# Loading expert weights in 32 KB stretches, with x transposed ahead of all experts

## The chip, the cores and the metric

The kernel runs on one core of one Trainium2 chip. The metric is the device time of one execution in microseconds, the median of several runs. Three runs of the kernel before gave 196.9, 197.62 and 198.62 us.

## What is computed

Eight experts, each a layer of two matrix products with a relu between them:

```python
n_experts, capacity, hidden, expert_hidden = 8, 256, 512, 2048
x:  (8, 256, 512) float32    w1: (8, 512, 2048) float32    w2: (8, 2048, 512) float32

h = np.matmul(x, w1)
h = np.maximum(h, 0)
return np.matmul(h, w2).astype(np.float32)
```

Each expert's two weight matrices hold 4.19 MB apiece in float32; x is 0.52 MB for each expert, and so is the output.

## The kernel before

One Python loop runs over the eight experts. All loads are issued from POOL's queue (GpSimd), which converts float32 to bfloat16 on the way; the outputs leave by SP's queue. A planner of dependencies places the semaphores; within each engine the order is that of the program.

For each expert:

- x arrives as a tile of 128 partitions with two rows of 512 each (line 57; the two rows lie side by side in memory). Eight 128x128 transposes on TensorE (line 63) go through two PSUM buffers, and VectorE copies each one to `xt_sb` (line 68).
- w1 arrives in one DMA (line 74). Its view `e (kt p) n -> e p kt n` gives partition p the rows p, 128 + p, 256 + p and 384 + p: four separate runs of 8 KB each. w2 arrives in two halves (lines 78 and 79); by its view partition p gets sixteen separate rows of 2 KB. The pool `moe_big` has two buffers of each, so the loads of expert e+2 wait until expert e has been worked off.
- The first layer (line 85): 16 tiles of 128 hidden units, each from four matmuls that accumulate, w1 stationary (128x128) and `xt_sb` moving (256 columns). ScalarE applies the relu and writes `ht_sb` (line 92).
- The second layer: `ht_sb` is stationary and w2 moving (512 columns). For each of two row tiles, eight matmuls accumulate over the first half of the hidden units (line 103) and eight over the second (line 117), in banks of their own. ScalarE copies the first half's sum to `out_sb` (line 111), VectorE adds the second (line 125), and SP stores the expert's 512 KB (line 127).

The identity for the transposes is made on POOL ahead of the loop (line 51; its instructions carry the lines of a helper, masks.py).

Of the kernel before, what the change touches and what calls it, by code (L numbers as in the profile page):

```python
# [1 line left out]

# [5 lines left out]


@with_exitstack
def kernel(
    ctx: ExitStack,
    tc: tile.TileContext,
    x: bass.AP,
    w1: bass.AP,
    w2: bass.AP,
    out: bass.AP,
):
    nc = tc.nc  # L20
    P = 128

    n_experts, capacity, hidden = x.shape
    _, _, expert_hidden = w1.shape

    M = capacity
    K1 = hidden
    K2 = expert_hidden
    N2 = hidden

    assert M % P == 0 and K1 % P == 0 and K2 % P == 0
    M_TILES = M // P
    K1_TILES = K1 // P
    K2_TILES = K2 // P

    bf = mybir.dt.bfloat16
    f32 = mybir.dt.float32

    x_r = x.rearrange("e (p mt) k -> e p mt k", p=P)
    w1_r = w1.rearrange("e (kt p) n -> e p kt n", p=P)  # L40
    w2_r = w2.rearrange("e (kt p) n -> e p kt n", p=P)
    out_r = out.rearrange("e (p mt) n -> e p mt n", p=P)

    big = ctx.enter_context(tc.tile_pool(name="moe_big", bufs=2))
    small = ctx.enter_context(tc.tile_pool(name="moe_small", bufs=3))
    psum_tr = ctx.enter_context(tc.tile_pool(name="moe_psum_tr", bufs=2, space=bass.MemoryType.PSUM))
    psum_mm = ctx.enter_context(tc.tile_pool(name="moe_psum_mm", bufs=6, space=bass.MemoryType.PSUM))
    const = ctx.enter_context(tc.tile_pool(name="moe_const", bufs=1))

    identity = const.tile([P, P], bf, name="identity")  # L50
    make_identity(nc, identity)

    HALF = K2_TILES // 2

    for e in range(n_experts):
        x_sb = small.tile([P, M_TILES, K1], bf, tag="x", name="x_sb")
        nc.gpsimd.dma_start(x_sb[:], x_r[e])  # L57

        xt_sb = small.tile([P, K1_TILES, M], bf, tag="xt", name="xt_sb")
        for mt in range(M_TILES):  # L60
            for kt in range(K1_TILES):
                pt = psum_tr.tile([P, P], bf, tag="ps_tr", name="pt_tr")
                nc.tensor.transpose(  # L63
                    pt[:],
                    x_sb[:, mt, kt * P:(kt + 1) * P],
                    identity[:],
                )
                nc.vector.tensor_copy(  # L68
                    xt_sb[:, kt, mt * P:(mt + 1) * P],
                    pt[:],  # L70
                )

        w1_sb = big.tile([P, K1_TILES, 16 * P], bf, tag="w1", name="w1_sb")
        nc.gpsimd.dma_start(w1_sb[:], w1_r[e])  # L74

        w2_a = big.tile([P, HALF, N2], bf, tag="w2a", name="w2_a")
        w2_b = big.tile([P, HALF, N2], bf, tag="w2b", name="w2_b")
        nc.gpsimd.dma_start(w2_a[:], w2_r[e, :, :HALF, :])  # L78
        nc.gpsimd.dma_start(w2_b[:], w2_r[e, :, HALF:, :])  # L79

        ht_sb = big.tile([P, K2_TILES, M], bf, tag="ht", name="ht_sb")
        for mt in range(K2_TILES):
            pt = psum_mm.tile([P, N2], f32, tag="ps_mm", name="pt_mm1")
            for kt in range(K1_TILES):
                nc.tensor.matmul(  # L85
                    pt[:, :M],
                    w1_sb[:, kt, mt * P:(mt + 1) * P],
                    xt_sb[:, kt, :],
                    start=(kt == 0),
                    stop=(kt == K1_TILES - 1),  # L90
                )
            nc.scalar.activation(  # L92
                ht_sb[:, mt, :], pt[:, :M],
                mybir.ActivationFunctionType.Relu,
            )

        out_sb = small.tile([P, M_TILES, N2], f32, tag="o", name="out_sb")
        pa = [None] * M_TILES
        pb = [None] * M_TILES
        for mt in range(M_TILES):  # L100
            pa[mt] = psum_mm.tile([P, N2], f32, tag="ps_mm", name="pt_mm2a")
            for kt in range(HALF):
                nc.tensor.matmul(  # L103
                    pa[mt][:],
                    ht_sb[:, kt, mt * P:(mt + 1) * P],
                    w2_a[:, kt, :],
                    start=(kt == 0),
                    stop=(kt == HALF - 1),
                )
        for mt in range(M_TILES):  # L110
            nc.scalar.activation(  # L111
                out_sb[:, mt, :], pa[mt][:],
                mybir.ActivationFunctionType.Identity,
            )
            pb[mt] = psum_mm.tile([P, N2], f32, tag="ps_mm", name="pt_mm2b")
            for kt in range(HALF):
                nc.tensor.matmul(  # L117
                    pb[mt][:],
                    ht_sb[:, HALF + kt, mt * P:(mt + 1) * P],
                    w2_b[:, kt, :],  # L120
                    start=(kt == 0),
                    stop=(kt == HALF - 1),
                )
        for mt in range(M_TILES):
            nc.vector.tensor_add(out_sb[:, mt, :], out_sb[:, mt, :], pb[mt][:])  # L125

        nc.sync.dma_start(out_r[e], out_sb[:])


# [1 line left out]
_INS = ['x', 'w1', 'w2']  # L131
_OUTS = [((8, 256, 512), 'float32')]


# [23 lines left out]
```

## Time and profile before

| | before |
|---|---|
| median of three runs | 197.62 us |
| the profiled execution's span | 197.5 us |
| its mean granted TensorE clock | 0.890 |
| TensorE matmuls, busy | 136.3 us (69%) |
| ScalarE, busy | 59.1 us |
| VectorE, busy | 22.4 us |
| load queue, share of 16 DMA engines | 99.8% |
| bytes read from HBM / written to HBM | 71.30 MB / 4.19 MB |

The profile is of one execution. Busy times of TensorE come from matmul records whose ends are modelled, so starts say more than durations. The rates of the windows count a load's bytes as they are written to SBUF, in bfloat16. A window's DMA share is the mean busy share of the 16 DMA engines; it can pass 1 because packets overlap. [...]

### The profile page before, as it was taken

How to read it: one execution, taken by the hardware profiler on the slowest of the kernel's cores; microseconds unless marked ns; L12 is line 12 of the kernel's file. 1: busy time of each engine (PE TensorE's matmuls, PEld its weight loads, DVE VectorE, ACT ScalarE, POOL GpSimd, SP SyncE). 2: the span in 40 equal slices, each digit the busy share in tenths (PEclk: the TensorE clock that was granted, in tenths of full speed). 3: DMA queues.
4: the chain of work that ended last, by engine and by line, in shares of the span. 5: the costliest groups of instructions: out<-in, count | busy, mean ns of one | idle time of the engine just before them, and what ended most of it. 6: DMA issues, size and time to landing. Idle time of an engine off the chain costs nothing.

```text
span 197.5 us, 2028 instructions
## 1 busy us (share of the span) xinstructions
PE 136.3 (69%) x824; PEld 87.9 (44%) x832; DVE 22.4 (11%) x80; ACT 59.1 (30%) x145; POOL 25.2 (13%) x38
## 2 busy tenths in 40 slices
PE   0304998159971999459970999519993699639990
PEld 0103853038530784248530684207741584227740
DVE  0200003100041000400040000500013000500011
ACT  2001741018400382018400382004720283005620
POOL 8700014000140002210230103100111000000000
PEclk9999999859997599969997599966999699966997
DMA  4999999999999999999999999999999999999402
GB/s 67 163 211 168 207 217 212 255 211 208 216 217 253 208 212 217 208 257 209 217 216 253 208 211 215 215 254 207 214 217 206 257 211 217 211 256 207 83 0 108
DMA packets 23177, 39.97 MB, mean 202 GB/s; under 512 B 640, under 2 KB 17024, under 8 KB 23168
## 3 DMA queue, kind: packets, MB, share of 16 engines
q0 software_dynamic: 22016, 35.65, 99.8%
q1 hardware_dynamic: 1152, 4.19, 5.6%
q8 instruction: 6, 0.10, 0.2%
q14 instruction: 3, 0.02, 0.0%
HBM read 71.30 MB, written 4.19 MB: 382 GB/s over the span
## 4 chain that ended last, share of the span: by engine, by line
DMA 72%; PE 13%; issue 10%; POOL 2%; DVE 0%; POOLq 0%; DVEq 0%
DMA w_sb<-in_w_dram 72%; PE pt_mm L85 9%; PE pt_mm2b L117 2%; PE pt_mm2a L103 2%; POOL x_sb L57 1%; POOL w_a L78 0%; POOL w_b L79 0%; POOL w_sb L74 0%; DVE out_sb L125 0%; POOL identity masks.py:199 0%; PE pt_tr L63 0%; POOL identity masks.py:197 0%; POOLq masks.py:199 0%; POOLq L74 0%; POOLq L78 0%
## 5 line engine op out<-in xcount | busy, mean ns | idle before, releaser
L85 PE MATMUL pt_mm<-xt_sb,w_sb 128*128 128x256 bf16 x512 | 72.7, 313 | 41.2 <-DMA w_sb<-in_w_dram 41.2
L85 PEld LDWEIGHTS <-w_sb 128*128 128x128 bf16 x512 | 56.6, 113 | 57.4 <-DMA w_sb<-in_w_dram 45.1
L92 ACT ACTIVATE ht_sb<-pt_mm 128x256 bf16<-128x256 f32 x128 | 48.3, 383 | 110.2 <-PE pt_mm L85 105.0
L117 PE MATMUL pt_mm2b<-w_b,ht_sb 128*128 128x512 bf16 x128 | 28.9, 379 | 0.0
L103 PE MATMUL pt_mm2a<-w_a,ht_sb 128*128 128x512 bf16 x120 | 28.5, 379 | 0.4
L125 DVE TENSOR_TENSOR out_sb<-out_sb,pt_mm2b 128x512 f32<-128x512 f32 x16 | 11.0, 688 | 126.7 <-PE pt_mm2b L117 118.9
L63 PE MATMUL pt_tr<-identity,x_sb 128*128 128x128 bf16 x64 | 12.1, 235 | 14.8 <-DVE xt_sb L68 9.6
L117 PEld LDWEIGHTS <-ht_sb 128*128 128x128 bf16 x128 | 12.5, 98 | 15.1
L103 PEld LDWEIGHTS <-ht_sb 128*128 128x128 bf16 x128 | 12.5, 98 | 13.4
L68 DVE COPY xt_sb<-pt_tr 128x128 bf16<-128x128 bf16 x64 | 12.0, 220 | 44.3 <-PE pt_tr L63 44.3
L74 POOL DMA_DIRECT2D w_sb<-in_w_dram x8 | 6.0, 754 | 80.0 <-PE pt_mm L85 80.0
L111 ACT ACTIVATE out_sb<-pt_mm2a 128x512 f32<-128x512 f32 x16 | 9.6, 597 | 19.8 <-PE pt_mm2a L103 19.8
L63 PEld LDWEIGHTS <-x_sb 128*128 128x128 bf16 x64 | 6.3, 105 | 18.3 <-issue 10.5
L78 POOL DMA_DIRECT2D w_a<-in_w_dram x8 | 7.1, 891 | 16.2 <-PE pt_mm2a L103 16.2
L79 POOL DMA_DIRECT2D w_b<-in_w_dram x8 | 7.1, 884 | 15.9 <-PE pt_tr L63 15.9
L57 POOL DMA_DIRECT2D x_sb<-in_x_dram x8 | 4.7, 582 | 12.1 <-PE pt_tr L63 11.7
L92 ACT ACT_TABLE_LOAD x1 | 1.3, 1283 | 0.7 <-PEq L142 0.7
masks.py:199 POOL TENSOR_SCALAR_AFFINE_SELECT identity<-identity 128x128 bf16<-128x128 bf16 x1 | 0.3, 304 | 0.1
masks.py:197 POOL MEMSET identity<- 128x128 bf16 x1 | 0.2, 204 | 0.3 <-POOLq L142 0.3
L142 POOL MEMSET const-float32-0.0<- 128x1 f32 x1 | 0.1, 98 | 0.2 <-issue 0.2
L142 POOL MEMSET const-bfloat16-1.0<- 128x1 bf16 x1 | 0.1, 101 | 0.0
L142 POOL MEMSET const-uint8-127<- 128x1 uint8 x1 | 0.1, 101 | 0.0
(1 smaller groups left out, 0.1 us busy)
## 6 DMA issues: line engine op xcount, KB each, us to landing
w_sb<-in_w_dram POOLq DMA_DIRECT2D x8, 2048.0 KB, 35.7
w_a<-in_w_dram POOLq DMA_DIRECT2D x8, 1024.0 KB, 38.1
w_b<-in_w_dram POOLq DMA_DIRECT2D x8, 1024.0 KB, 39.7
out_dram<-out_sb SPq DMA_DIRECT2D x8, 512.0 KB, 6.3
x_sb<-in_x_dram POOLq DMA_DIRECT2D x8, 256.0 KB, 37.0
```

Source lines behind the costliest of these rows:

```text
L57: nc.gpsimd.dma_start(x_sb[:], x_r[e])
L63: nc.tensor.transpose(pt[:], x_sb[:, mt, kt * P:(kt + 1) * P], identity[:],)
L68: nc.vector.tensor_copy(xt_sb[:, kt, mt * P:(mt + 1) * P], pt[:],)
L74: nc.gpsimd.dma_start(w1_sb[:], w1_r[e])
L78: nc.gpsimd.dma_start(w2_a[:], w2_r[e, :, :HALF, :])
L79: nc.gpsimd.dma_start(w2_b[:], w2_r[e, :, HALF:, :])
L85: nc.tensor.matmul(pt[:, :M], w1_sb[:, kt, mt * P:(mt + 1) * P], xt_sb[:, kt, :], start=(kt == 0), stop=(kt == K1_TILES - 1),)
L92: nc.scalar.activation(ht_sb[:, mt, :], pt[:, :M], mybir.ActivationFunctionType.Relu,)
L103: nc.tensor.matmul(pa[mt][:], ht_sb[:, kt, mt * P:(mt + 1) * P], w2_a[:, kt, :], start=(kt == 0), stop=(kt == HALF - 1),)
L111: nc.scalar.activation(out_sb[:, mt, :], pa[mt][:], mybir.ActivationFunctionType.Identity,)
L117: nc.tensor.matmul(pb[mt][:], ht_sb[:, HALF + kt, mt * P:(mt + 1) * P], w2_b[:, kt, :], start=(kt == 0), stop=(kt == HALF - 1),)
L125: nc.vector.tensor_add(out_sb[:, mt, :], out_sb[:, mt, :], pb[mt][:])
```

## The change

- The rows of each weight matrix go to the partitions in another order: `e (p kt) n -> e p kt n`, so partition p gets rows 4p to 4p+3 of w1 and rows 16p to 16p+15 of w2. Each partition then loads one contiguous stretch of 32 KB in float32 of either matrix. Every matrix comes in one DMA, but for the last expert's w2, which comes in four pieces of 6, 5, 3 and 2 row tiles.
- x is loaded whole, ahead of the weights: partition p gets sixteen consecutive rows, 32 KB. The identity is made on POOL after the first expert's loads have been issued.
- All 64 transposes run ahead of the experts, eight to a PSUM bank. Since hidden row p*4 + kt lies in partition p of tile kt, a transpose reads every fourth column of x (`kt::KT1`); VectorE and ScalarE take turns in copying eight transposes at once into `xt_sb`, which now holds all experts, with a permutation of the columns.
- By the same order the first layer reads its stationary tiles from w1 with a step of sixteen columns (`2 * g + i::KT2`). Two tiles of 256 columns share a bank, and the relu of 512 columns goes to ScalarE and VectorE in turn.
- The second layer accumulates all sixteen tiles in one bank for each row tile, the two row tiles alternating. VectorE copies one and ScalarE the other to `out_sb`. The last expert's output leaves in two halves, by SP's and ScalarE's queues.
- Four buffers of each weight matrix instead of two.

```diff
--- before.py
+++ after.py
@@ -1,4 +1,3 @@
-
 from contextlib import ExitStack
 
 import concourse.bass as bass
@@ -19,112 +18,111 @@
 ):
     nc = tc.nc
     P = 128
-
-    n_experts, capacity, hidden = x.shape
-    _, _, expert_hidden = w1.shape
-
-    M = capacity
-    K1 = hidden
-    K2 = expert_hidden
-    N2 = hidden
-
-    assert M % P == 0 and K1 % P == 0 and K2 % P == 0
-    M_TILES = M // P
-    K1_TILES = K1 // P
-    K2_TILES = K2 // P
-
     bf = mybir.dt.bfloat16
     f32 = mybir.dt.float32
 
-    x_r = x.rearrange("e (p mt) k -> e p mt k", p=P)
-    w1_r = w1.rearrange("e (kt p) n -> e p kt n", p=P)
-    w2_r = w2.rearrange("e (kt p) n -> e p kt n", p=P)
+    E, C, H = x.shape
+    F = w1.shape[2]
+    MT = C // P
+    KT1 = H // P
+    KT2 = F // P
+    J = E * C // P
+    PL = P // E
+    J2 = J // MT
+
+
+    x_r = x.rearrange("e c k -> (e c) k").rearrange("(p j) k -> p j k", p=P)
+    w1_r = w1.rearrange("e (p kt) n -> e p kt n", p=P)
+    w2_r = w2.rearrange("e (p kt) n -> e p kt n", p=P)
     out_r = out.rearrange("e (p mt) n -> e p mt n", p=P)
 
-    big = ctx.enter_context(tc.tile_pool(name="moe_big", bufs=2))
-    small = ctx.enter_context(tc.tile_pool(name="moe_small", bufs=3))
-    psum_tr = ctx.enter_context(tc.tile_pool(name="moe_psum_tr", bufs=2, space=bass.MemoryType.PSUM))
-    psum_mm = ctx.enter_context(tc.tile_pool(name="moe_psum_mm", bufs=6, space=bass.MemoryType.PSUM))
-    const = ctx.enter_context(tc.tile_pool(name="moe_const", bufs=1))
+    const = ctx.enter_context(tc.tile_pool(name="const", bufs=1))
+    wpool = ctx.enter_context(tc.tile_pool(name="weights", bufs=4))
+    hpool = ctx.enter_context(tc.tile_pool(name="hidden", bufs=2))
+    opool = ctx.enter_context(tc.tile_pool(name="outs", bufs=3))
+    ps_h = ctx.enter_context(tc.tile_pool(name="ps_h", bufs=4, space=bass.MemoryType.PSUM))
+    ps_o = ctx.enter_context(tc.tile_pool(name="ps_o", bufs=4, space=bass.MemoryType.PSUM))
 
-    identity = const.tile([P, P], bf, name="identity")
-    make_identity(nc, identity)
+    x_sb = const.tile([P, J, H], bf, name="x_sb")
+    nc.gpsimd.dma_start(x_sb[:], x_r)
 
-    HALF = K2_TILES // 2
+    w1_sb, w2_sb = [], []
+    for e in range(E):
+        a = wpool.tile([P, KT1, F], bf, tag="w1", name="w1_sb")
+        nc.gpsimd.dma_start(a[:], w1_r[e])
+        b = wpool.tile([P, KT2, H], bf, tag="w2", name="w2_sb")
+        if e < E - 1:
+            nc.gpsimd.dma_start(b[:], w2_r[e])
+        else:
+            for lo, hi in ((0, 6), (6, 11), (11, 14), (14, 16)):
+                nc.gpsimd.dma_start(b[:, lo:hi, :], w2_r[e, :, lo:hi, :])
+        w1_sb.append(a)
+        w2_sb.append(b)
+        if e == 0:
+            identity = const.tile([P, P], bf, name="identity")
+            make_identity(nc, identity)
 
-    for e in range(n_experts):
-        x_sb = small.tile([P, M_TILES, K1], bf, tag="x", name="x_sb")
-        nc.gpsimd.dma_start(x_sb[:], x_r[e])
 
-        xt_sb = small.tile([P, K1_TILES, M], bf, tag="xt", name="xt_sb")
-        for mt in range(M_TILES):
-            for kt in range(K1_TILES):
-                pt = psum_tr.tile([P, P], bf, tag="ps_tr", name="pt_tr")
+    xt_sb = const.tile([P, KT1, E, C], bf, name="xt_sb")
+    n = 0
+    for mt in range(MT):
+        for kt in range(KT1):
+            pt = ps_o.tile([P, J2, P], bf, tag="ps_o", name="pt_tr")
+            for j2 in range(J2):
                 nc.tensor.transpose(
-                    pt[:],
-                    x_sb[:, mt, kt * P:(kt + 1) * P],
-                    identity[:],
+                    pt[:, j2, :], x_sb[:, j2 * MT + mt, kt::KT1], identity[:]
                 )
-                nc.vector.tensor_copy(
-                    xt_sb[:, kt, mt * P:(mt + 1) * P],
-                    pt[:],
+            src = pt[:].rearrange("p j (e l) -> p e l j", e=E)
+            dst = xt_sb[:, kt, :, mt * P:(mt + 1) * P].rearrange(
+                "p e (l j) -> p e l j", j=J2
+            )
+            if n % 2:
+                nc.scalar.copy(dst, src)
+            else:
+                nc.vector.tensor_copy(dst, src)
+            n += 1
+
+    for e in range(E):
+        ht_sb = hpool.tile([P, KT2, C], bf, tag="ht", name="ht_sb")
+        for g in range(KT2 // 2):
+            pt = ps_h.tile([P, 2, C], f32, tag="ps_h", name="pt_h")
+            for i in range(2):
+                for kt in range(KT1):
+                    nc.tensor.matmul(
+                        pt[:, i, :],
+                        w1_sb[e][:, kt, 2 * g + i::KT2],
+                        xt_sb[:, kt, e, :],
+                        start=(kt == 0),
+                        stop=(kt == KT1 - 1),
+                    )
+            if g % 2:
+                nc.vector.tensor_relu(ht_sb[:, 2 * g:2 * g + 2, :], pt[:])
+            else:
+                nc.scalar.activation(
+                    ht_sb[:, 2 * g:2 * g + 2, :], pt[:],
+                    mybir.ActivationFunctionType.Relu,
                 )
 
-        w1_sb = big.tile([P, K1_TILES, 16 * P], bf, tag="w1", name="w1_sb")
-        nc.gpsimd.dma_start(w1_sb[:], w1_r[e])
-
-        w2_a = big.tile([P, HALF, N2], bf, tag="w2a", name="w2_a")
-        w2_b = big.tile([P, HALF, N2], bf, tag="w2b", name="w2_b")
-        nc.gpsimd.dma_start(w2_a[:], w2_r[e, :, :HALF, :])
-        nc.gpsimd.dma_start(w2_b[:], w2_r[e, :, HALF:, :])
-
-        ht_sb = big.tile([P, K2_TILES, M], bf, tag="ht", name="ht_sb")
-        for mt in range(K2_TILES):
-            pt = psum_mm.tile([P, N2], f32, tag="ps_mm", name="pt_mm1")
-            for kt in range(K1_TILES):
+        po = [
+            ps_o.tile([P, H], f32, tag="ps_o", name=f"pt_o{mt}") for mt in range(MT)
+        ]
+        for kt in range(KT2):
+            for mt in range(MT):
                 nc.tensor.matmul(
-                    pt[:, :M],
-                    w1_sb[:, kt, mt * P:(mt + 1) * P],
-                    xt_sb[:, kt, :],
+                    po[mt][:],
+                    ht_sb[:, kt, mt * P:(mt + 1) * P],
+                    w2_sb[e][:, kt, :],
                     start=(kt == 0),
-                    stop=(kt == K1_TILES - 1),
+                    stop=(kt == KT2 - 1),
                 )
-            nc.scalar.activation(
-                ht_sb[:, mt, :], pt[:, :M],
-                mybir.ActivationFunctionType.Relu,
-            )
-
-        out_sb = small.tile([P, M_TILES, N2], f32, tag="o", name="out_sb")
-        pa = [None] * M_TILES
-        pb = [None] * M_TILES
-        for mt in range(M_TILES):
-            pa[mt] = psum_mm.tile([P, N2], f32, tag="ps_mm", name="pt_mm2a")
-            for kt in range(HALF):
-                nc.tensor.matmul(
-                    pa[mt][:],
-                    ht_sb[:, kt, mt * P:(mt + 1) * P],
-                    w2_a[:, kt, :],
-                    start=(kt == 0),
-                    stop=(kt == HALF - 1),
-                )
-        for mt in range(M_TILES):
-            nc.scalar.activation(
-                out_sb[:, mt, :], pa[mt][:],
-                mybir.ActivationFunctionType.Identity,
-            )
-            pb[mt] = psum_mm.tile([P, N2], f32, tag="ps_mm", name="pt_mm2b")
-            for kt in range(HALF):
-                nc.tensor.matmul(
-                    pb[mt][:],
-                    ht_sb[:, HALF + kt, mt * P:(mt + 1) * P],
-                    w2_b[:, kt, :],
-                    start=(kt == 0),
-                    stop=(kt == HALF - 1),
-                )
-        for mt in range(M_TILES):
-            nc.vector.tensor_add(out_sb[:, mt, :], out_sb[:, mt, :], pb[mt][:])
-
-        nc.sync.dma_start(out_r[e], out_sb[:])
+        out_sb = opool.tile([P, MT, H], f32, tag="o", name="out_sb")
+        nc.vector.tensor_copy(out_sb[:, 0, :], po[0][:])
+        nc.scalar.copy(out_sb[:, 1, :], po[1][:])
+        if e < E - 1:
+            nc.sync.dma_start(out_r[e], out_sb[:])
+        else:
+            nc.sync.dma_start(out_r[e, :, 0, :], out_sb[:, 0, :])
+            nc.scalar.dma_start(out_r[e, :, 1, :], out_sb[:, 1, :])
 
 
 # ---- launch: one core; inputs and outputs as the reference has them ----
```

## Rows read from the trace of the kernel before

**Rows 1.** The page: span, matmuls, all DMA packets, and the load queue's.

```profile
span 197.5 us, 2028 instructions
PE 136.3 (69%) x824; PEld 87.9 (44%) x832; DVE 22.4 (11%) x80; ACT 59.1 (30%) x145; POOL 25.2 (13%) x38
...
DMA packets 23177, 39.97 MB, mean 202 GB/s; under 512 B 640, under 2 KB 17024, under 8 KB 23168
...
q0 software_dynamic: 22016, 35.65, 99.8%
```

**Rows 2.** The chain that ended last, in order: start us, us, what.

```profile
5.34 36.50 DMA w_sb<-in_w_dram
...
142.27 33.56 DMA w_sb<-in_w_dram
...
189.19 3.47 PE pt_mm2b L117 x16
...
192.75 0.69 DVE out_sb L125
```

**Rows 3.** Windows: length, busy times, PEclk, DMA share, GB/s; two of w2, two of w1.

```profile
43.00:48.00 5.00, 5.00 (x40) 4.13 (x38) 0.00 (x0) 3.42 (x10) 0.00 (x0) 0.82 1.24 207
157.00:161.00 4.00, 4.00 (x37) 3.48 (x36) 0.00 (x0) 3.25 (x9) 0.00 (x0) 0.95 1.24 206
53.00:59.00 6.00, 4.95 (x26) 2.31 (x25) 2.00 (x6) 0.60 (x1) 2.18 (x3) 1.00 1.06 215
165.00:171.00 6.00, 5.22 (x26) 2.38 (x25) 1.47 (x4) 1.16 (x2) 0.00 (x0) 1.00 1.07 216
```

**Rows 4.** Windows, columns as before: the two slow stretches of the start.

```profile
2.50:9.00 6.50, 1.59 (x8) 0.76 (x8) 1.43 (x8) 0.00 (x0) 5.93 (x8) 1.00 0.93 147
...
15.00:19.00 4.00, 1.61 (x8) 1.18 (x9) 0.00 (x0) 0.38 (x1) 0.00 (x0) 1.00 1.07 159
```

**Rows 5.** Windows from one landing of w1 to the next: first and seventh.

```profile
17.39:41.88 24.49, 16.73 (x102) 10.79 (x103) 2.58 (x9) 7.32 (x18) 3.06 (x4) 0.92 1.15 219
...
154.64:175.87 21.23, 16.44 (x103) 10.70 (x104) 2.80 (x10) 7.21 (x18) 0.00 (x0) 0.90 1.14 222
```

**Rows 6.** Timeline, last two experts: start us, us, engine, line, operation, count, idle before.

```profile
163.04 3.62 PE L103 MATMUL pt_mm2a<-w_a,ht_sb 128*128 128x512 bf16 x15
...
175.87 0.13 PEld L85 LDWEIGHTS <-w_sb 128*128 128x128 bf16 x2 [4.02 <-DMA w_sb<-in_w_dram]
...
176.38 9.35 PE L85 MATMUL pt_mm<-xt_sb,w_sb 128*128 128x256 bf16 x62
...
185.57 3.62 PE L103 MATMUL pt_mm2a<-w_a,ht_sb 128*128 128x512 bf16 x15
```

**Rows 7.** Windows, columns as before, in the last expert.

```profile
175.00:176.00 1.00, 0.12 (x1) 0.13 (x2) 0.00 (x0) 0.00 (x0) 0.00 (x0) 0.50 1.08 330
...
183.00:184.00 1.00, 1.00 (x12) 0.90 (x10) 0.00 (x0) 0.86 (x3) 0.00 (x0) 1.00 1.11 185
...
184.00:187.00 3.00, 2.95 (x22) 2.09 (x22) 0.00 (x0) 1.92 (x5) 0.00 (x0) 1.00 0.31 51
```

**Rows 8.** Timeline: two transposes in a row, two weight loads of MM1.

```profile
169.94 0.22 PE L63 MATMUL pt_tr<-identity,x_sb 128*128 128x128 bf16 x1
170.00 0.22 PE L63 MATMUL pt_tr<-identity,x_sb 128*128 128x128 bf16 x1
...
183.17 0.10 PEld L85 LDWEIGHTS <-w_sb 128*128 128x128 bf16 x1
183.28 0.10 PEld L85 LDWEIGHTS <-w_sb 128*128 128x128 bf16 x1
```

**Rows 9.** The page's groups: evictions of 512 columns; busy us, mean ns.

```profile
L125 DVE TENSOR_TENSOR out_sb<-out_sb,pt_mm2b 128x512 f32<-128x512 f32 x16 | 11.0, 688 | 126.7 <-PE pt_mm2b L117 118.9
...
L111 ACT ACTIVATE out_sb<-pt_mm2a 128x512 f32<-128x512 f32 x16 | 9.6, 597 | 19.8 <-PE pt_mm2a L103 19.8
```

**Rows 10.** Timeline of POOL at the start.

```profile
1.27 0.69 POOL L57 DMA_DIRECT2D x_sb<-in_x_dram  x1 [0.33 <-issue]
```

## The prediction

> **What bounds the kernel now.** I read the page first: 16 DMA engines at 99.8% with packets of the load queue, TensorE at 69% [rows 1]. The queue's 35.65 MB are counted as they arrive, in bfloat16; they are read from HBM as float32, so a rate in the windows (bytes written to SBUF) stands for twice that rate of reading. Then the chain of waits in order of time: four waits for a w1 transfer cover most of it, each from its issue to its landing, 34 to 38 us (the first and the last stand in [rows 2]). So the load queue always holds more than one expert's work, and what counts is how fast it drains. The last w1 lands at 175.87, and from there TensorE decides: the first layer (MM1 below) 175.87 to 185.57, the second (MM2) to 192.66, the add to 193.44, the output DMA to the end at 197.5. That tail is 21.6 us, although little of the loads is left at 184 (51 GB/s over the next 3 us) [rows 1, 2, 6, 7].
>
> Last, the windows, stage by stage. While w2 lands the queue moves 206 to 207 GB/s, while w1 lands 215 to 216 [rows 3]; I know which is which from where the stage lies: what follows the landing of a w1 is that expert's w2. In the first 19 us two stretches are slower, 147 and 159 GB/s [rows 4]. From then on an expert takes 21.2 to 24.5 us, in which TensorE is busy for 16.4 to 17.5 us (the first and the seventh of the seven periods are in [rows 5]); before the last MM1 its weight loads stood idle for 4.0 us [rows 6].
>
> **Larger descriptors.** The packet count tells the form: 22016 packets of the load queue [rows 1] are 4096 for w1 (8 KB read, 4 KB written), 16384 for w2 (2 KB read), 1024 for x (4 KB read) and 512 for the completions of 32 DMAs. So a packet is one contiguous run, and one of 32 KB should be one packet too. By [rows 3] an engine needs 16 x 2048 / 414 = 79.1 ns for a w2 packet and 16 x 8192 / 430 = 304.8 ns for a w1 packet. Two points, one line: 27.2 bytes per ns and 3.9 ns for each packet. A packet of 32 KB then takes 1204 + 3.9 ns, which is 434 GB/s of reading. w2 of one expert (4.19 MB) falls from 10.13 to 9.66 us, w1 from 9.75 to 9.66, x from 1.24 to 1.21. Ahead of the last w1 lie seven w2, eight w1 and eight x: 7 x 0.47 + 8 x 0.09 + 8 x 0.03 = 4.2 us earlier. Bounds: nothing, if bytes alone set the pace and w2 is slower for another reason; and no more than that line gives, since w1 at 430 is within 1% of it. I take 4.2, because the two stages differ in nothing that I can see but the run length.
>
> **The start.** The first load is now the first thing POOL does after its constants; before, it was issued at 1.27, behind the first step of the identity [rows 10]. I take 0.6 us earlier; 0 to 1.0 are the bounds. The two slow stretches cost (207 - 147) x 6.5 + (207 - 159) x 4 = 582 KB, or 2.8 us [rows 4]. In the first of them POOL is writing descriptors for most of the time; there will be an eighth or a quarter as many per weight. I don't know that this is the cause; bounds 0 and 2.8, I take 0.9.
>
> **x first.** The bytes are the same; only their order changes. x (9.7 us) now stands ahead of the first w1, which lands at about 2.0 + 9.7 + 9.7 + 1.9 of the start's loss + about 1 for the slowest engine = 24.4 instead of 17.39. TensorE starts 7 us later and that costs nothing, since what it lacks at each expert is data. The 64 transposes move into the 9.7 us in which w1 of expert 0 arrives. Their eight evictions of 1024 columns with a stepped pattern have no row; by the 512-column rows [rows 9] they take 1.2 us (ACT) and 1.4 us (DVE), or twice that if the steps cost, and each engine has four: 5 to 11 us. If that spills past w1's landing, the 4 us that TensorE idles in each expert take it up by the third.
>
> **Four experts in flight.** Worth 0 by itself: the queue never emptied [rows 1, 2]. POOL's waits get harmless: the load of expert e+4 waits for MM1 of expert e, everything behind it on POOL is another load, and some 60 us of transfers are queued ahead.
>
> **The weight loads with a step.** w1's stationary tiles are now read with a step of 16 elements (32 bytes), the x tiles with 8 bytes. No row shows a weight load with a step. What the rows show of contiguous ones: two transposes, each with its own weights, start 0.06 us apart at granted clock 1.00, while MM1's weight loads, and so its matmuls, start 0.11 us apart at that clock [rows 3, 7, 8]. So a contiguous load takes at most 0.06 of the 0.11 us that hide it. Twice that, 0.12, would add 0.01 us to a matmul or 0.5 us to MM1; three times, 0.17, some 2.8 us, counting only the 44 or so of 64 matmuls that run at the higher clock; lower bound nothing. I take a cost near nothing, 0.15 us, as the nearest row leaves a factor of two. [...]
>
> **The tail.** MM1 took 9.70 us for the last expert and 8.40 for the one before (154.64 to 163.04) [rows 5, 6], mean 9.05; a stray transpose among its first matmuls goes, 0.1: 8.95, with the step 9.1. The granted clock is 0.50 when TensorE restarts after its 4 us of idling [rows 7], and I expect it so again. MM2 stays 32 matmuls, 7.1. One relu of 512 columns per 8 matmuls (0.88 us) alternates between ACT (0.60) and DVE (0.69) [rows 9]; it hides. MM2 now accumulates all 16 tiles in one bank, so the two ACT copies go and the closing add becomes a copy of the same size: 0.8 with its latency. The output is halved onto two queues: 4.06 falls to some 3.7; between 3.4 and 4.1. Cutting the last w2 in four gains nothing that shows: w2's last piece lands about 10 us after w1, TensorE reaches its tiles 15 us after it. Tail: 9.1 + 7.1 + 0.8 + 3.7 = 20.7.
>
> **The output before the last.** Expert 6's output ran just ahead of the last w1 (330 GB/s around its landing [rows 7], where loads alone move 215) and took up to 1.2 us (0.52 MB at 430 GB/s) from it. With periods of 20.5 us (two weights and an output) and 17 us of TensorE work it comes later or at the same moment: I take half, 0.6.
>
> **Sum.** The last w1 lands at 175.87 - 4.2 - 0.6 - 0.9 - 0.6 = 169.6, and the span is 169.6 + 20.7 = 190.3. The profiled span of 197.5 stands beside a median of 197.62, so nothing is added: 190.3.
>
> **Rivals.**
> Rate unchanged (0.12): bytes set the pace, and the start stays as slow. 175.87 - 0.6 + 20.7 = 196.0, with the collision 195.4. For it: w1 at 8 KB already runs within 1% of the line. Against: the 4% between w1 and w2 are in every expert.
> The start and the lag go too (0.16): when the last w1 has landed, w2 is already 2 us ahead on the faster engines (2.1 MB take 9.7 us, and at 184, 8.1 us later, little is left [rows 7]), so the slowest engine runs late; if fewer descriptors mend this and the whole 2.8: 190.3 - 1.9 - 1.5 = 186.9; if the lag goes whole, the first load starts a further 0.4 earlier and the output is clear of w1, 184.9.
> The step costs some (0.13): weight loads of 0.17 us give MM1 11.7 instead of 9.1, still under the transfers: 192.9.
> The step makes TensorE the bound (0.07), the one that ends slower: place MM1, price per weight load. The period of 20.5 is passed when 64 loads take 13.4 us, 0.21 each. Beyond that the end is 24.4 + 8 x (64 loads + 7.1) + 4.5; it equals 197.5 at 0.218 us a load, and at four times 0.06 it is 208.6. Against it: it needs a factor of 3.6 over a bound that may itself be loose. [...]
> Long packets are slower (0.06): a packet occupies its engine four to sixteen times as long, and neighbouring partitions read from addresses 32 KB apart; 5% less rate adds 8 us to the sum: 198.3. No row speaks for it.
> The forecast has 0.46, 188 to 192.5.
>
> **Chances and range.** About 1% is what a measurement of this kernel can tell from no change: faster means under 195.6. Faster: 0.46 + 0.16 + 0.13 and a quarter of the unchanged rate, 0.78. Same: the rest of that and a little of the slow cases, 0.11. Slower: 0.11. The range runs from 185, near the floor of the second rival, to 196.5, which takes in the unchanged rate and leaves out the two slow cases.
>
> **What would show it.** The windows while w2 lands should read 217 GB/s, like those of w1, in some 2900 packets instead of 22016. The first w1 should land near 24, the last near 170, with 20.5 us between neighbours and TensorE idle before each. MM1's matmuls at the higher clock should start 0.11 us apart; 0.12 to 0.17 is the third rival, 0.21 and no idle time the fourth. The tail after the last w1 should be 20.7. I am wrong if w2's windows stay at 207, if weight loads take over MM1, or if w1 of expert 7 lands before 167.

## The result

The changed kernel takes 189.14 us (median of 4 runs, 189.05 to 189.31) beside 198.02 us for the kernel before on the same chip (4 runs, 196.9 to 198.62): a ratio of 0.958, with a 95% interval of 0.952 to 0.963. The forecast was 190.3, with a range of 185 to 196.5.

The profiled execution of the changed kernel has a span of 187.0 us, 10.5 less than that of before. Its page, beside [rows 1]; the lines are the span, the engines' busy time, all DMA packets, and the load queue's packets, MB and share of 16 engines:

```profile
span 187.0 us, 1874 instructions
PE 133.5 (71%) x832; PEld 91.0 (49%) x832; DVE 32.6 (17%) x44; ACT 29.1 (16%) x45; POOL 11.4 (6%) x26
...
DMA packets 4182, 39.95 MB, mean 214 GB/s; under 512 B 464, under 2 KB 464, under 8 KB 2128
...
q0 software_dynamic: 2880, 35.65, 90.1%
```

The same bytes come in 2880 packets of the load queue instead of 22016. The windows of the two early stretches and of one whole period, beside [rows 4, 5] (length, busy times, granted clock, DMA share, GB/s):

```profile
2.50:9.00 6.50, 0.00 (x0) 0.00 (x0) 0.00 (x0) 0.00 (x0) 3.54 (x8) 1.00 1.06 202
...
15.00:19.00 4.00, 4.00 (x41) 4.00 (x39) 2.97 (x3) 2.02 (x2) 0.00 (x0) 1.00 0.92 197
...
147.60:168.29 20.69, 15.96 (x96) 10.50 (x97) 3.46 (x5) 2.97 (x5) 0.00 (x0) 0.92 1.00 224
```

The slow stretches went from 147 and 159 GB/s to 202 and 197, and an expert takes 20.1 to 20.9 us where it took 21.2 to 24.5. With the long packets, windows of 1 us scatter from 131 to 262 GB/s between 10 and 20 us, so the rates of short windows are loose, and the sign that the prediction named, 217 GB/s while w2 lands, can't be read in them. Whole periods from one landing of w1 to the next can be compared: 220 to 228 GB/s with the output in them, and 215 for the two weights alone, if the output takes the 1.2 us that the prediction gave it. The timeline of the weight loads of the first layer (MM1), the last second layer (MM2) and the end, beside [rows 6]; the last column is the idle time before, and what ended it:

```profile
23.67 8.35 PEld L91 LDWEIGHTS <-w_sb 128*128 128x128 bf16 x64 [3.36 <-DMA w_sb<-in_w_dram]
...
168.29 6.97 PEld L91 LDWEIGHTS <-w_sb 128*128 128x128 bf16 x64 [1.53 <-DMA w_sb<-in_w_dram]
...
175.33 7.07 PE L111 MATMUL pt_o<-w_sb,ht_sb 128*128 128x512 bf16 x32
...
182.44 0.59 ACT L120 COPY out_sb<-pt_o 128x512 f32<-128x512 f32 x1 [7.18 <-PE pt_o L111]
182.94 0.33 SPq L124 DMA_DIRECT2D out_dram<-out_sb  x1
```

The last w1 lands at 168.29, 7.6 us earlier than before, and the tail behind it takes 18.7 us instead of 21.6, 2.9 less. Together these are the 10.5 us between the two profiled executions. By the medians of the time the change gains 8.9 us: the profiled execution of before was a long one (197.5 us, where 21 others have spans with a median of 195.6), so every comparison with its landings below is too kind by up to 1.9 us.

### The profile page after: what moved, and what is told of

The parts are those of the page before. It is cut to its first block, busy times and chain, and to the rows that moved or that the text cites. A ratio compares the mean times of both kernels' runs of the same rounds, so it can differ in the third digit from the quotient of the medians.

```text
span 187.0 us, 1874 instructions
## 1 busy us (share of the span) xinstructions
PE 133.5 (71%) x832; PEld 91.0 (49%) x832; DVE 32.6 (17%) x44; ACT 29.1 (16%) x45; POOL 11.4 (6%) x26
## 3 DMA queue, kind: packets, MB, share of 16 engines
q0 software_dynamic: 2880, 35.65, 90.1%
## 4 chain that ended last, share of the span: by engine, by line
PE 60%; DMA 22%; another core or an unknown queue 14%; issue 1%; POOL 1%; ACT 0%; POOLq 0%
PE pt_o L111 32%; PE pt_h L91 28%; DMA w_sb<-in_w_dram 22%; POOL x_sb L47 0%; ACT out_sb L120 0%; POOL w_sb L52 0%; POOL identity masks.py:197 0%; POOL w_sb L55 0%; POOLq L140 0%
## 5 line engine op out<-in xcount | busy, mean ns | idle before, releaser
L111 PE MATMUL pt_o<-w_sb,ht_sb 128*128 128x512 bf16 x256 | 66.7, 426 | 22.3 <-DMA w_sb<-in_w_dram 22.3
L91 PE MATMUL pt_h<-xt_sb,w_sb 128*128 128x256 bf16 x512 | 60.6, 281 | 12.6 <-DMA w_sb<-in_w_dram 12.6
L99 DVE TENSOR_SCALAR ht_sb<-pt_h 128x512 bf16<-128x512 f32 x32 | 22.1, 692 | 52.4 <-PE pt_h L91 52.4
L101 ACT ACTIVATE ht_sb<-pt_h 128x512 bf16<-128x512 f32 x32 | 19.1, 597 | 46.6 <-PE pt_h L91 46.6
L119 DVE COPY out_sb<-pt_o 128x512 f32<-128x512 f32 x8 | 5.5, 692 | 81.6 <-PE pt_o L111 81.6
L120 ACT COPY out_sb<-pt_o 128x512 f32<-128x512 f32 x8 | 4.7, 588 | 91.0 <-PE pt_o L111 91.0
L72 PE MATMUL pt_tr<-identity,x_sb 128*128 128x128 bf16 x64 | 6.5, 296 | 14.0 <-DMA x_sb<-in_x_dram 14.0
L72 PEld LDWEIGHTS <-x_sb 128*128 128x128 bf16 x64 | 6.3, 141 | 14.0 <-DMA x_sb<-in_x_dram 14.0
L82 DVE COPY xt_sb<-pt_tr 128x1024 bf16<-128x1024 bf16 x4 | 4.9, 1225 | 16.4 <-PE pt_tr L72 16.4
L52 POOL DMA_DIRECT2D w_sb<-in_w_dram x8 | 4.4, 544 | 44.3 <-PE pt_h L91 44.3
L80 ACT COPY xt_sb<-pt_tr 128x1024 bf16<-128x1024 bf16 x4 | 4.0, 1012 | 15.5 <-PE pt_tr L72 15.5
L55 POOL DMA_DIRECT2D w_sb<-in_w_dram x7 | 3.8, 546 | 38.7 <-PE pt_o L111 30.5
L58 POOL DMA_DIRECT2D w_sb<-in_w_dram x4 | 2.1, 532 | 32.0 <-DMA w_sb<-in_w_dram 19.3
```

Source lines behind the costliest of these rows:

```text
L52: nc.gpsimd.dma_start(a[:], w1_r[e])
L55: nc.gpsimd.dma_start(b[:], w2_r[e])
L58: nc.gpsimd.dma_start(b[:, lo:hi, :], w2_r[e, :, lo:hi, :])
L72: nc.tensor.transpose(pt[:, j2, :], x_sb[:, j2 * MT + mt, kt::KT1], identity[:])
L80: nc.scalar.copy(dst, src)
L82: nc.vector.tensor_copy(dst, src)
```

## The experiments

Each kernel below was timed beside the kernel before, in four runs where not said otherwise; landings are of the profiled execution.

**The long runs alone.** The kernel before with other views, and the steps that these need:

```diff
-    w1_r = w1.rearrange("e (kt p) n -> e p kt n", p=P)
-    w2_r = w2.rearrange("e (kt p) n -> e p kt n", p=P)
+    w1_r = w1.rearrange("e (p kt) n -> e p kt n", p=P)
+    w2_r = w2.rearrange("e (p kt) n -> e p kt n", p=P)
...
-                    x_sb[:, mt, kt * P:(kt + 1) * P],
+                    x_sb[:, mt, kt::K1_TILES],
...
-                    w1_sb[:, kt, mt * P:(mt + 1) * P],
+                    w1_sb[:, kt, mt::K2_TILES],
```

> The kernel before with one thing changed: the views of w1 and w2, so that each partition's share of a load is one run (32 KB for w1, 16 KB for each half of w2), with the stepped reads that this order needs on TensorE. Order of loads, two buffers, transposes per expert and the tail stay. Theory of the runs (3.9 ns for each packet): w2 windows rise from 207 to 216 GB/s, the last w1 lands 4.1 us earlier than 175.87, at 171.8, and by up to 2.8 us more if the two slow stretches of the start go with the short packets; tail 21.5; span 190.5 to 193.3. Rival, order and depth make the gain (x first, four experts in flight) and the transfers are set by bytes: span 196.5 to 198.

Measured: 193.96 us, ratio 0.980 (0.975 to 0.985), span 192.8. Its start and its last landing:

```profile
2.50:9.00 6.50, 1.59 (x8) 0.81 (x8) 1.43 (x8) 0.00 (x0) 4.02 (x8) 1.00 0.99 169
...
171.31 0.21 PEld L85 LDWEIGHTS <-w_sb 128*128 128x128 bf16 x2 [2.22 <-DMA w_sb<-in_w_dram]
```

The last w1 lands 4.6 us earlier than in the profiled execution of before; the tail is 21.5. The four spans are 190.7 to 192.8, all within the theory of the runs and none near its rival's 196.5. The runs alone give a ratio of 0.980, about half of what the whole change gives.

**w2 back in short rows.** The changed kernel with w2's old view, and so with contiguous weight tiles:

```diff
-    w2_r = w2.rearrange("e (p kt) n -> e p kt n", p=P)
+    w2_r = w2.rearrange("e (kt p) n -> e p kt n", p=P)
...
-                        w1_sb[e][:, kt, 2 * g + i::KT2],
+                        w1_sb[e][:, kt, (2 * g + i) * P:(2 * g + i + 1) * P],
```

> The changed kernel with w2 back in rows of 2 KB (sixteen to a partition), and so with the first layer's weight tiles contiguous again; w1 and x keep their 32 KB runs, x stays first, four buffers stay. Theory of the runs: 0.47 us more for each of seven w2 ahead of the last w1, which lands at 171.6 instead of 168.3; span 190.3, more if the start slows again. Rival, order and depth: 187, as the changed kernel.

Measured: 193.39 us, span 191.1.

```profile
2.50:9.00 6.50, 0.00 (x0) 0.00 (x0) 0.00 (x0) 0.00 (x0) 5.49 (x8) 1.00 1.07 202
...
23.59 8.55 PEld L91 LDWEIGHTS <-w_sb 128*128 128x128 bf16 x64 [4.24 <-DMA w_sb<-in_w_dram]
...
172.47 6.88 PEld L91 LDWEIGHTS <-w_sb 128*128 128x128 bf16 x64 [0.61 <-DMA w_sb<-in_w_dram]
```

The first w1 lands when it does in the changed kernel, the last 4.2 us later (172.47 against 168.29): 0.6 us for each of seven w2. That is 120 more packets per engine and w2, so 5.0 ns each, where the two windows of before had given 3.9.

**w2 in runs of 8 KB.** The changed kernel with four runs to a partition; the last w2 comes in four equal pieces, where the changed kernel has 6, 5, 3 and 2 row tiles:

```diff
-    w2_r = w2.rearrange("e (p kt) n -> e p kt n", p=P)
+    w2_r = w2.rearrange("e (a p k) n -> e p a k n", a=4, p=P)
...
-                        w1_sb[e][:, kt, 2 * g + i::KT2],
+                        w1_sb[e][:, kt, ((2 * g + i) // 4) * 512 + (2 * g + i) % 4:((2 * g + i) // 4 + 1) * 512:4],
```

> The changed kernel with w2 in four runs of 8 KB to a partition instead of one of 32 KB (and w1's tiles read with a step of 4 instead of 16). If a fixed time for each packet is what short runs cost, the 2 KB rows' 4.2 us over seven w2 are 120 packets each at 5 ns, and 8 KB means 24 packets: 0.8 us, last w1 at 169.1, span 187.8. If rows of 2 KB are slow for a reason of their own: no loss, 187.0, or one that does not follow the packets, 189 and more.

Measured: 190.04 us (190.01 to 190.08), span 187.7.

```profile
169.03 6.96 PEld L91 LDWEIGHTS <-w_sb 128*128 128x128 bf16 x64 [0.25 <-DMA w_sb<-in_w_dram]
```

169.1 and 187.8 were expected of a fixed time for each packet, so the loss follows the number of packets. TensorE is only just done with expert 6 when this w1 lands, which makes the landing a loose one; expert 6's w2, for which TensorE has long been waiting, starts its layer at 159.35 instead of 158.50, 0.85 later, where 24 packets at 5.0 ns in seven w2 make 0.84.

**x first.** The kernel of the long runs with x in one DMA ahead of the weights, in runs of 4 KB:

```diff
+    x_all = const.tile([P, n_experts, M_TILES, K1], bf, name="x_all")
+    nc.gpsimd.dma_start(x_all[:], x.rearrange("e (p mt) k -> p e mt k", p=P))
     for e in range(n_experts):
-        x_sb = small.tile([P, M_TILES, K1], bf, tag="x", name="x_sb")
-        nc.gpsimd.dma_start(x_sb[:], x_r[e])
...
-                    x_sb[:, mt, kt::K1_TILES],
+                    x_all[:, e, mt, kt::K1_TILES],
```

> The kernel before with w1 and w2 in long runs (as in the run that changed only the views) and x in one DMA ahead of all weights, in runs of 4 KB; transposes stay with their expert. Theory that the order mends the start: the last w1 moves from 171.3 to some 169.3, span 190.8. Rival, the order is worth nothing and the start's slow stretches have another cause: last w1 at 171.3, span 192 to 193.

Measured: 192.56 us (190.75 to 193.18), span 190.0, the last w1 at 170.00, between the two expectations; the spans, 188.7 to 191.3, are nearer to the first. Its start, with the landing of x as the wait of the transposes, and that wait in the changed kernel (L72):

```profile
2.50:9.00 6.50, 0.00 (x0) 0.00 (x0) 0.00 (x0) 0.00 (x0) 3.34 (x7) 1.00 0.97 158
...
15.31 0.24 PEld L64 LDWEIGHTS <-x_all 128*128 128x128 bf16 x3 [15.31 <-DMA x_all<-in_x_dram]
...
24.96 9.27 PEld L86 LDWEIGHTS <-w_sb 128*128 128x128 bf16 x64 [2.54 <-DMA w_sb<-in_w_dram]
...
13.99 6.33 PEld L72 LDWEIGHTS <-x_sb 128*128 128x128 bf16 x64 [13.99 <-DMA x_sb<-in_x_dram]
```

The first w1 lands 1.3 us later than in the changed kernel, which has x first too, but in runs of 32 KB, and the first stretch moves 158 GB/s against its 202. So being first is not enough. Nor is it that POOL is busy with issuing loads: with w2 in short rows POOL was busy for 5.49 of the 6.5 us, and the stretch had its 202. All of the 1.3 us are lost in x's own transfer, which lands at 15.31 instead of 13.99; w1 follows 9.7 us behind in both. An estimate explains about half: POOL takes 0.4 us longer to issue x (1.03 us against 0.66), and 56 more packets for each engine at 5.0 ns are 0.3. What makes the rest is not shown; that the fast starts make the identity behind the first loads was not separated from the long runs of x. The times of this kernel and of that with the long runs alone scatter by 2 us and overlap, so the gain of the order between them (1.4 us by the medians) is loosely known. From here to the changed kernel are another 3.4 us by the medians; between the two traces the last w1 makes 1.7 and the tail 1.3 (20.0 against 18.7).

**Two buffers.** `bufs=4` of the weights' pool set to 2.

> The changed kernel with two buffers of each weight matrix instead of four. Theory of the runs: the load queue holds about one expert's work even so and never empties; span 187, within 0.5. Rival, depth makes a part of the gain: 189 or more, with stretches of low GB/s after the landing of a weight.

Measured: 189.04 us (188.95 to 189.18), span 186.7, the last w1 at 167.99. Depth is worth nothing here.

**The last w2 uncut.** The last expert's w2 in one DMA like the others:

```diff
-        if e < E - 1:
+        if e < E:
             nc.gpsimd.dma_start(b[:], w2_r[e])
```

> The changed kernel with the last expert's w2 in one DMA instead of four. Theory after the result: the second layer of the last expert starts when its first piece is there, right after the first layer, and would otherwise wait for the whole, to about 179 instead of 175.4; span 187 + 3.5 = 190.5. Rival, the prediction's word that the cut gains nothing that shows: 187.

Measured: 194.3 us, span 191.8, 4.8 us longer than the changed kernel's. The matmuls of its end, and the window from MM2's start:

```profile
167.97 7.21 PE L91 MATMUL pt_h<-xt_sb,w_sb 128*128 128x256 bf16 x64 [1.33 <-DMA w_sb<-in_w_dram]
178.71 0.58 PE L111 MATMUL pt_o<-w_sb,ht_sb 128*128 128x512 bf16 x1 [3.53 <-DMA w_sb<-in_w_dram]
...
178.70:182.00 3.30, 3.06 (x8) 1.20 (x9) 0.00 (x0) 0.00 (x0) 0.00 (x0) 0.55 0.00 0
```

TensorE waits 3.5 us for the whole w2 and then restarts at a granted clock of 0.50 (179 to 181 us; 0.55 over that window), which costs the rest: MM2 takes 8.5 us instead of 7.1.

**All w2 in halves.** The first seven w2 in two DMAs each:

```diff
-            nc.gpsimd.dma_start(b[:], w2_r[e])
+            for lo, hi in ((0, 8), (8, 16)):
+                nc.gpsimd.dma_start(b[:, lo:hi, :], w2_r[e, :, lo:hi, :])
```

> The changed kernel with every w2 of the first seven experts in two DMAs of half the tiles. Theory of the clock: the second layer then starts with the first half, TensorE is done some 3 us sooner with each expert and idles before the next w1 instead of before w2; the last first layer restarts at a granted clock of 0.50 and takes 8.5 to 9.7 us instead of 7.2, with the last w1 landing where it did (168.3, up to 0.6 later for expert 6's earlier output): span 188.3 to 190. Rival, the first layer of the last expert is short because of the stepped reads or the shared relu, not because of where TensorE idles: 7.2 as now, span 187 within 0.6.

Measured: 191.76 us (191.16 to 192.06), span 189.7. The last first layer and the clock around it:

```profile
168.54 9.72 PE L92 MATMUL pt_h<-xt_sb,w_sb 128*128 128x256 bf16 x64 [3.99 <-DMA w_sb<-in_w_dram]
...
168.00:172.00 4.00, 3.46 (x17) 2.68 (x18) 0.00 (x0) 0.60 (x1) 0.00 (x0) 0.50 1.01 256
```

w1 lands 0.25 us later (8 more packets for each engine, in each of seven w2, make 0.28 at 5.0 ns), and MM1 takes 9.7 us instead of 7.2, at a granted clock of 0.50 at first, after 4.0 us of idling. TensorE has sooner finished expert 6 and waits longer for w1; that earlier finish is paid back at the lower clock. So the changed kernel's short last MM1 comes from where TensorE idles, not from the matmuls.

**The price of a step.** Three rows of 128 matmuls behind the changed kernel's end, 64 moving columns each, reading weights contiguously (line 131), with a step of 4 (line 135) and of 16 (line 139):

```diff
+    for n in range(128):
+        nc.tensor.matmul(pt[:, 0, :64], wt[:, n % 4, (n % 16) * P:(n % 16) * P + P], mv,
+                         start=True, stop=True)
...
+        nc.tensor.matmul(pt[:, 0, :64], wt[:, n % 4, n % 4:n % 4 + 4 * P:4], mv,
+                         start=True, stop=True)
...
+        nc.tensor.matmul(pt[:, 0, :64], wt[:, n % 4, n % 16::16], mv,
+                         start=True, stop=True)
```

> The changed kernel with three rows of 128 matmuls added behind its end, each matmul with a weight tile of its own and only 64 moving columns, so that the weight load is not hidden: the first row reads its weights contiguously, the second with a step of 4 elements, the third with a step of 16. Their results are not used. If a stepped load costs nothing, the three rows have one distance from start to start, at most the 0.06 us seen between two transposes. [...]

One execution. The timeline of the matmuls (start us, us), at a granted clock of 1.00 throughout:

```profile
182.16 3.90 PE L131 MATMUL pt_s<-xt_sb,w_sb 128*128 128x64 bf16 x128
185.89 4.43 PE L135 MATMUL pt_s<-xt_sb,w_sb 128*128 128x64 bf16 x128
190.15 8.10 PE L139 MATMUL pt_s<-xt_sb,w_sb 128*128 128x64 bf16 x128
```

From the first start of a row to that of the next are 3.73 and 4.26 us, 29 and 33 ns a matmul; the third row, 8.1 us long, has some 62 ns. With the step of 16 a load takes at least twice as long as a contiguous one (with 64 columns the contiguous row may be held by the matmuls, so 29 ns is only a bound on its load). The contiguous load is at least twice as fast as the prediction's bound of 60 ns.

**The end cut finer.** To see whether the tail can shrink: expert 6's w2 in halves, expert 7's w1 in two column halves, its w2 in pieces that follow.

```diff
+            for h in range(2):
+                nc.gpsimd.dma_start(
+                    a[:, :, h * FH:(h + 1) * FH], w1_r[e, :, :, h * FH:(h + 1) * FH]
+                )
...
+                        wt = w1_sb[e][:, kt, h * FH + t % 8:(h + 1) * FH:8]
```

> The changed kernel with the end cut finer: expert 6's w2 in two halves, expert 7's w1 in two halves of its columns (runs of 4 KB), expert 7's w2 in four pieces that follow the same halves of the hidden units. If the end is set by how late the last first layer can start, it now starts with half of w1: the second layer ends about 1 us behind the last load (178.7 to 179), span 184 to 185. Rival: TensorE restarts at a granted clock of 0.50 and gives most of that back, span 186.5 to 187.

Measured: 192.26 us, span 189.9, longer by 2.9 us than the changed kernel's, and worse than either expectation.

```profile
163.54 0.33 PE L110 MATMUL pt_h<-xt_sb,w_sb 128*128 128x256 bf16 x1 [1.34 <-DMA w_sb<-in_w_dram]
169.82 8.65 PE L110 MATMUL pt_h<-xt_sb,w_sb 128*128 128x256 bf16 x63 [5.96 <-DMA w_sb<-in_w_dram]
...
170.00:171.00 1.00, 1.00 (x6) 0.78 (x6) 0.00 (x0) 0.00 (x0) 0.00 (x0) 0.50 1.31 291
```

The first matmul starts with the first half; the second waits 6 us for the other half, which by the code it doesn't read, and TensorE comes back at a granted clock of 0.50. The halves interleave in each partition (every row of the tile is half one and half the other), and the planner seems to take them for overlapping; that is inferred, and the next run bears it out. The mended version stores each piece as one block, and cuts w1 in four:

```diff
+            aq = a[:].rearrange("p k f -> p (k f)").rearrange(
+                "p (q k f) -> p q k f", q=4, k=KT1
+            )
+            for q in range(4):
+                nc.gpsimd.dma_start(aq[:, q], w1_r[e, :, :, q * FQ:(q + 1) * FQ])
...
+            w2_q = w2[e].rearrange("(q p k) n -> q p k n", q=4, p=P)
+            for q, lo, hi in ((0, 0, 4), (1, 0, 4), (2, 0, 4), (3, 0, 2), (3, 2, 4)):
...
+                        wt = aq[:, t // 4, kt, t % 4::4]
```

> As the run that cut the last expert finer, with the last w1 in four quarters of its columns, each quarter stored as one block of the tile, so that the planner of dependencies can tell the pieces apart; the last w2 in five pieces that follow the quarters. Theory: what spoiled that run was the wait of the second matmul for the whole w1; now the first layer follows the quarters from about 161 on, the second layer ends about 1 us after the last load (179.3, the runs of 2 and 8 KB cost 0.6): span 184.7 to 185.7. Rival, the idle time between the pieces drops the granted clock to 0.50 again: 186.5 to 188.

Measured: 187.84 us (187.73 to 188.03), ratio to the kernel before 0.950 (0.943 to 0.956), span 185.4.

```profile
161.83 3.66 PE L110 MATMUL pt_h<-xt_sb,w_sb 128*128 128x256 bf16 x32
166.01 1.94 PE L110 MATMUL pt_h<-xt_sb,w_sb 128*128 128x256 bf16 x16 [0.53 <-DMA w_sb<-in_w_dram]
169.90 1.94 PE L110 MATMUL pt_h<-xt_sb,w_sb 128*128 128x256 bf16 x16 [1.95 <-DMA w_sb<-in_w_dram]
172.38 1.89 PE L130 MATMUL pt_o<-w_sb,ht_sb 128*128 128x512 bf16 x8 [0.54 <-DMA w_sb<-in_w_dram]
174.81 1.89 PE L130 MATMUL pt_o<-w_sb,ht_sb 128*128 128x512 bf16 x8 [0.55 <-DMA w_sb<-in_w_dram]
177.26 3.61 PE L130 MATMUL pt_o<-w_sb,ht_sb 128*128 128x512 bf16 x16 [0.56 <-DMA w_sb<-in_w_dram]
...
161.00:181.00 20.00, 15.75 (x101) 10.20 (x99) 3.76 (x6) 3.06 (x6) 0.53 (x1) 1.00 1.00 197
```

Both layers now follow the pieces with waits of 0.5 to 2.0 us, and the matmuls keep the higher clock (1.00 over these 20 us). This is the fastest of the kernels tried: its four spans are 185.4 to 185.7 where those of the changed kernel are 186.8 to 187.0, though the intervals of the two ratios overlap.

**The last output by one queue.** The device time exceeds the span by 1.7 to 1.8 us in the runs of the kernel before, and by 2.2 to 2.3 in the changed one. The second half of the last output on SP's queue instead of ScalarE's:

```diff
-            nc.scalar.dma_start(out_r[e, :, 1, :], out_sb[:, 1, :])
+            nc.sync.dma_start(out_r[e, :, 1, :], out_sb[:, 1, :])
```

> The changed kernel with both halves of the last output on SP's queue. In the runs so far device time minus span is 1.8 us for the kernel before and 2.2 to 2.3 for the changed one. Theory: the use of ScalarE's DMA queue adds the 0.45; then 1.8 here, with the span at 187.0 to 187.5. Rival: the gap stays at 2.2 and belongs to something else that changed.

Measured: 189.04 us, span 186.8: still 2.2. The theory falls, and what the 0.45 us are stays open. In the kernel with x first in runs of 4 KB, which uses SP's queue alone, the gap is 1.8 to 2.05, so a part of it may come with the order of the loads. The second queue brings nothing either.

## Why the prediction was right, and where its steps were not

The direction, the size and the main mechanism, a fixed time for each packet, came out as forecast, but the nearness of 190.3 to 189.14 is in part luck: 190.3 was the sum of a span, and the span is 187.0. Two errors of about 2 us offset each other, a starting span that was too long and a distance from span to time that was put at nothing. The gain that the sum had was 7.2 us; by the medians it is 8.9.

- **What lies around the span** was set to nothing, because the profiled span of before (197.5) stood beside a median time of 197.62. That step failed. Of the 21 executions of the kernel before that ran beside these experiments, all but one have spans of 194.7 to 197.4, and the times are 1.7 to 1.8 us longer; the profiled one was a long one, by about 2 us, and that hid what lies around. The changed kernel's own time lies 2.2 us above its span.
- **Larger descriptors**: right, and a little undersized. 3.3 us were expected of seven w2, 4.2 were measured by putting their short rows back; 5.0 ns a packet in place of 3.9. The runs of 8 KB fell on the same line. The period is 20.7 us, against 20.5. The rival that short rows are slow for a reason of their own falls with the 8 KB.
- **The start**: 0.6 us for issuing sooner did not come, since the first load is issued at 1.23 instead of 1.27 [rows 10]; POOL is held up there by something else (0.78 us idle just ahead of it). But the slow stretches gave back (202 - 147) x 6.5 + (197 - 159) x 4 = 510 KB, about 2.4 of the 2.8 us, where 0.9 was taken. That is within the bounds that the prediction set, and loose: it is read against the one trace of before, a long execution, and with w1's own share (8 x 24 packets, 1.0 us) the measured parts add to the 7.6 us between the two traces, not to the smaller gain between typical executions. The cause that the prediction offered, that POOL is writing descriptors, is not it: with w2 in short rows one issue of w2 takes POOL 1.18 us, where it takes 0.55 in the changed kernel, and POOL was busy for 5.49 of the 6.5 us, yet the stretch stayed fast. The cause stays open.
- **The first w1** lands at 23.67 (24.4 forecast), **the last** at 168.29 (169.6). An estimate for a typical execution of before: if the 1.9 us by which the profiled one is long lie ahead of the last w1 (the tail is 21.6 us there and 21.5 with the long runs alone), its landing gained 5.7 us, where 6.3 were forecast. The evictions of the transposes take 1.23 us on DVE and 1.01 on ACT, a little under the lower bounds.
- **Four experts in flight** were worth nothing, as argued: two buffers give the same time. Behind x and seven weight loads, POOL's eighth weight load waits 8.13 us, by the profile for x to land, and nothing is lost by that either.

```profile
14.23 0.54 POOL L55 DMA_DIRECT2D w_sb<-in_w_dram  x1 [8.13 <-DMA x_sb<-in_x_dram]
```

- **The weight loads with a step**: 0.15 us were taken, and 0.09 show: the 64 loads of the last MM1 take 6.97 us, and 6.88 with contiguous tiles (w2 in short rows). In the added rows the step of 16 costs: some 62 ns from start to start against 29 with contiguous columns, and 33 with a step of 4. That doesn't reach the time, since MM1's matmuls start 0.11 us apart (64 in the 7.04 us from 168.29 to 175.33), and 62 ns are hidden in that.
- **The tail** was oversized: 20.7 against 18.7. Nearly all of it is MM1, 9.1 against 7.2. The step that failed is "the granted clock is 0.50 when TensorE restarts after its 4 us of idling, and I expect it so again". The idle time moved: with w2 in one piece expert 6's MM2 now waits 3.7 us for it and then loses more at a granted clock that falls to 0.50 on the way (160 to 163 us; 8.75 us instead of 7.1), so that TensorE is done later with expert 6, waits only 1.5 us for the last w1, and meets it at 1.00. The run with all w2 in halves moves the idle time back and gets the old MM1 of 9.7 us. The wait alone doesn't settle the clock: expert 5's MM2 waited 3.9 us, and its whole period, 126.70 to 147.60, shows 1.00. The windows below are the first 4.5 us of expert 6's MM2 and the last MM1:

```profile
158.50:163.00 4.50, 4.50 (x14) 1.78 (x14) 0.00 (x0) 0.00 (x0) 0.00 (x0) 0.63 1.05 224
...
168.29:175.50 7.21, 7.21 (x65) 7.13 (x66) 2.08 (x3) 2.39 (x4) 0.00 (x0) 1.00 1.04 246
```

- **"Cutting the last w2 in four gains nothing that shows"** compared with the two halves of before and overlooked the neighbour that it replaces: uncut, it costs 4.8 us. The tail of 18.7 rests on that cut.
- **The output before the last** was put at 0.6 us. No run sizes it: it is issued at 167.91 now, 0.4 us ahead of the landing, and in the run with halves, where it leaves at 165.20, the 0.25 us by which the last w1 is later are no more than the added packets make.
- Of **the rivals**, "rate unchanged" is refuted by the two runs of w2, a TensorE bound by the step by the waits that it still shows for every weight, long packets being slower by the periods. "The start and the lag go too" came half true: the start did, for the most part. (Its floor of 184.9 does not come out of the terms that are given: 1.9, the whole lag of 2, 0.4 and 0.6 off 190.3 make 185.4.)

## What to carry to other kernels

Where a queue is busy all the time, count its packets. A fixed time for each, read off two stages with different run lengths, forecast here what longer runs bring (3.9 ns read off, 5.0 measured). Reordering a weight's rows so that each partition reads one run was worth it here, where the stepped reads hid behind the matmuls (some 62 ns in 0.11 us). Look at the last item apart from the steady state: which piece it waits for, and whether the engine that will run it has just been idle, decided most of the 2.9 us that the tail lost here (MM1 9.7 us before, 7.2 now). Compare a profiled span with other executions' spans, not with a time, before adding nothing for what lies around it.

## What the runs showed of the hardware that was not expected

- At a granted clock of 1.00, matmuls of 64 columns with a 128x128 bfloat16 weight load each start 29 ns apart with contiguous columns (so the load takes no more), 33 ns with a step of 8 bytes, and some 62 ns with a step of 32 bytes.
- With x first, the first 6.5 us moved 202 GB/s where x came in runs of 32 KB and 158 where it came in runs of 4 KB, and x landed 1.3 us later. The number of packets and the longer issue explain about half of that by estimate; the rest is open.
- Splitting transfers so that TensorE starts sooner can lengthen the kernel (189.14 us with the first seven w2 whole, 191.76 with them in halves), because here the idle time lands ahead of the stage that sets the end, and that stage restarts at a granted clock of 0.50 (9.7 us instead of 7.2).
